# Queueing the casts of x and the first weight splits behind the PSUM copies of p's projections, in a hybrid decoder block on one Trainium2 core

## The chip, the core and the metric

The kernel runs on one core of one Trainium2 chip. The core has a matrix engine (TensorE, PE in the profile; PEld are its weight loads), VectorE (DVE), ScalarE (ACT), GpSimd (POOL) and SyncE (SP), which here only issues transfers. Matmul results land in PSUM, of which the kernel uses eight banks: four under the tag "g", four under "s". The metric is device time in microseconds, and lower is better.

## The reference

One layer of a decoder block on 256 tokens of width 2048, all in float32:

```
h = RMSNorm(x);  u = h @ W_in            # 12288 columns: c b xa za q f iv og ga gb
yA = (B * conv3(C * xa)) * silu(zA)      # short convolution
yB = HGRN2(silu(q), f, iv) normed * silu(og)
m  = sigmoid(ga) * (yA @ W_A) + sigmoid(gb) * (yB @ W_B);  x = x + m @ W_o
x  = x + sigmoid(RMSNorm(x) @ W_pg) * (p @ W_pp);  out = RMSNorm(x)
```

The last but one product, p @ W_pp (256 tokens, 256 deep, 2048 wide), depends on inputs alone, and this kernel computes it first.

## The kernel before

**Products.** A float32 matrix is used as two float32r parts, a rounded one (hi) and what is left (lo), and a product is three matmuls: hi by hi, hi by lo, lo by hi (`product`, lines 898 to 900). For weights, ScalarE makes the hi part (`whi`, line 123) and VectorE the lo part (`wlo`, line 124), in `split`. For x, `put` makes `xh` on ScalarE (line 215, which also applies the norm's gain) and `xl` on VectorE (line 216). In this text a cast is ScalarE's half of that, a split VectorE's.

**Positions and groups.** The weights are one stream of positions; a position is 256 rows by 512 columns of a weight matrix (512 KB) and takes 12 matmuls of 128x512: three for each of two row blocks and two token blocks. A group is 512 output columns, and uses two PSUM banks, one for each token block. Groups 0 to 3 are p's projections ("PP"), one position each (positions 0 to 3). Then come the input groups of eight positions each, the first at positions 4 to 11 (`FIRST = 4`), whose epilogue is `ep_f`. Projections 0 and 1 take all four "g" banks, projections 2 and 3 take "s" banks, and all input groups take "g" banks. So the first input group needs the banks of projection 0, the second those of projection 1.

**The copies.** The epilogue of a projection (`ep_pp`, lines 702 to 708) copies one bank out on ScalarE (line 704) and one on VectorE (line 705) to a tile, shown as `t`, and two steps later SP stores the tile to DRAM (`pw_d`, line 708). It is read back only with the last four groups (`load_pw`).

**The order.** Loop `for pos` first prepares weights until three positions ahead (`ahead`, LEAD = 3), then issues the position's matmuls, then lets each active epilogue go one step (`advance`). From position 4 on, preparing a position `done` also prepares two pieces of x (`put_x`, 128 features each, sixteen in all). The framework's scheduler then orders each engine's queue by its own estimates; an engine works through its queue strictly in that order. `tc.issue_after(i)` makes what is issued inside it stand behind instruction `i` on the engine that they share. `step` uses it so that an epilogue's instructions stand behind the last split. Before the change nothing tells the scheduler how the copies stand to the casts of x.

**Buffers and transfers.** `raw` holds two positions in each of three buffers, so positions 10 and 11 are loaded into the buffer of 4 and 5, and so on; `whi` and `wlo` have four buffers each, so position q's cast waits for the matmuls of position q - 4. SP issues all transfers in order: the first weights, x in eight pieces, weights of positions 6 to 9, then the stores to `pw_d`, further weights, four loads of x by tokens (`load_tokens`, line 802) and small masks (lines 943 and 944). The built program also lets a transfer wait for the landing of one eight before it.

**The norm of x.** ScalarE sums squares of the four token loads (`add_squares`, line 806), VectorE and GpSimd make rstd1 from it, and only then can `ep_f(0)` read the first group's banks (line 265), at position 18.

Of the kernel before, what the change touches and what calls it, by code (L numbers as in the profile page):

```python
# [11 lines left out]
AF = mybir.ActivationFunctionType  # L12
# [7 lines left out]
KT = D // P  # L20
# [3 lines left out]
CW = 512  # L24
# [21 lines left out]
def hybrid_kernel(ctx, tc, xT, x, pT, prm, gfin, masks, w_in, w_a, w_b, w_o, w_pg, w_pp, out):  # L46
    nc = tc.nc
# [11 lines left out]
    def open_pool(name, side):  # L59
        closers[name] = ExitStack()  # L60
        pools[name] = closers[name].enter_context(
            tc.tile_pool(name=name, bufs=1, side=side, reuse_waits="tile")
        )

    def close_pool(name):
        closers.pop(name).close()
        del pools[name]
# [3 lines left out]
    state = {"tmp": "tmp1"}  # L71
# [3 lines left out]
    def nm(s):  # L75
        uid[0] += 1
        return f"{s}_{uid[0]}"

    def t4(tag="t4", bufs=None):
        bufs = bufs or {"tmp1": 8, "tmp2": 5, "tmp3": 5}[state["tmp"]]  # L80
        return pools[state["tmp"]].tile([P, 1024], F32, tag=tag, bufs=bufs, name=nm(tag))
# [13 lines left out]
    def raw_of(pos):  # L95
        q = pos // 2
        if q not in loaded:
            loaded[q] = wp.tile([P, 2, 2 * CW], F32, tag="raw", bufs=3, name=nm("raw"))
        return loaded[q]

    def load(pos):
        q = pos // 2
        if q not in loaded:
            raw = raw_of(pos)
            w, g, c = stream[2 * q]
            if q < APART // 2:
                for i in range(2):
                    w, g, c = stream[2 * q + i]
                    nc.sync.dma_start(out=raw[:, i, :], in_=w[g, :, c, :])
            else:  # L110
                nc.sync.dma_start(out=raw, in_=w[g, :, c : c + 2, :])

    def split(pos, halves=(0, 1)):
        load(pos)
        src = raw_of(pos)[:, pos % 2, :]
        pool, n = (pools["late"], 6) if pos >= gate and (pos - gate) % 10 >= 4 else (wp, 4)
        if pos not in parts:
            parts[pos] = tuple(
                pool.tile([P, 2 * CW], F32R, tag=tag, bufs=n, name=nm(tag)) for tag in ("whi", "wlo")
            )  # L120
        hi, lo = parts[pos]
        s = slice(halves[0] * CW, (halves[-1] + 1) * CW)
        a = nc.scalar.activation(out=hi[:, s], in_=src[:, s], func=AF.Copy)  # L123
        v = nc.vector.tensor_tensor(  # L124
            out=lo[:, s], in0=src[:, s], in1=hi[:, s].bitcast(F32), op=ALU.subtract
        )
        state["splits"] = (a.ins, v.ins)
# [19 lines left out]
    FIRST = 4  # L147
# [11 lines left out]
    def load_x(k, n):  # L159
        nc.sync.dma_start(  # L160
            out=xraw[k // 4].rearrange("p (k t) -> p k t", k=4)[:, k % 4 : k % 4 + n, :], in_=xT[:, k : k + n, :]
        )
# [38 lines left out]
    def gain(base, k):  # L201
        return prm_t[:, base + k : base + k + 1]
# [5 lines left out]
    def put(op, k, src, scale=None):  # L208

        hi, lo = op[0][:, k, :], op[1][:, k, :]  # L210
        if scale is None:
            nc.scalar.activation(out=hi, in_=src, func=AF.Copy)
            nc.vector.tensor_tensor(out=lo, in0=src, in1=hi.bitcast(F32), op=ALU.subtract)
        else:
            nc.scalar.activation(out=hi, in_=src, func=AF.Identity, scale=scale)  # L215
            nc.vector.scalar_tensor_tensor(
                out=lo, in0=src, scalar=scale, in1=hi.bitcast(F32), op0=ALU.mult, op1=ALU.subtract
            )
# [482 lines left out]

    def ep_pp(j, psum):
        pw = t4()
        nc.scalar.activation(out=pw[:, :CW], in_=psum[0], func=AF.Copy)  # L704
        nc.vector.tensor_copy(out=pw[:, CW:], in_=psum[1])
        yield
        yield
        nc.sync.dma_start(out=pw_d[:, j, :], in_=pw)

    def load_pw(j):  # L710
        state["pw", j] = t4("pw", 2)
        nc.sync.dma_start(out=state["pw", j], in_=pw_d[:, j, :])
# [79 lines left out]
    def put_x(k):  # L792
        put(state["hT"], k, xraw[k // 4][:, (k % 4) * T : (k % 4 + 1) * T], gain(PRM_GMIX, k))
# [10 lines left out]
    def add_squares(q):  # L804

        tc.keep_in_program_order(nc.scalar.activation(
            out=xtok[q], in_=xtok[q], func=AF.Square, accum_out=state["ss1"][:, q : q + 1]
        ))

    def norm_of_x():  # L810
        tot = sc(NT, "tot1", 1)
        nc.vector.tensor_reduce(
            out=tot, in_=state["ss1"].rearrange("p (t h) -> p t h", t=NT),
            axis=mybir.AxisListType.X, op=ALU.add,
        )
        r = state["rstd1"] = rsqrt_of(tot, NT, D, "r1")
        state["rstd1_2"] = sc(NT, "r1s", 1)
        nc.vector.tensor_tensor(out=state["rstd1_2"], in0=r, in1=r, op=ALU.mult)
# [39 lines left out]
    def put_p(k):  # L858
        put(state["pT"], k, praw[:, k * T : (k + 1) * T])
# [14 lines left out]
    def step(e):  # L874

        a, v = state["splits"]
        with tc.issue_after(a), tc.issue_after(v):
            try:
                next(e)
            except StopIteration:  # L880
                active.remove(e)
# [9 lines left out]
    def ahead(pos):  # L891

        return LEAD + min(max(pos - gate, 0) // 4, 5)
# [9 lines left out]
    psum = None  # L903
    done = 0
    for pos, (gi, c) in enumerate(steps[:last_group]):
        kind, j, w, g, opname = groups[gi]
        nch = w.shape[2]
        if pos == gate:
            close_pool("m")
            open_pool("late", "left")  # L910
        while done < min(pos + 1 + ahead(pos), len(steps)):
            if done < 2:
                for i in range(2):
                    if done == 0:
                        put_p(i)
                    split(done, (i,))
            else:
                for k in range(2 * (done - FIRST), min(2 * (done - FIRST) + 2, KT)) if done >= FIRST else ():
                    put_x(k)
                split(done)  # L920
            done += 1
        if pos == 0:
            load(FIRST + 2)
            for k in (8, 10):
                load_x(k, 2)
            load(FIRST + 4)
            for k in (12, 14):
                load_x(k, 2)
        if pos >= gate and c == 0:
            load_pw(j)  # L930
        if pos == FIRST + 4:
            begin()
        if 0 <= pos - NORM < 4:
            add_squares(pos - NORM)
        if pos == NORM + 3:
            norm_of_x()
        if pos == NORM + 4:
            active.append(ep_f(0, waiting))
            step(active[-1])
            nc.gpsimd.memset(full_m, 0)  # L940
            for i in range(4):
                z = slice(i * Q, (i + 1) * Q)
                nc.sync.dma_start(out=near_m[z], in_=masks[z, :NARROW, z])
                nc.sync.dma_start(out=full_m[z, :, z], in_=masks[z, NARROW:, z])
        if c == 0:
            psum = [bank("s" if kind == "PP" and j >= 2 else "g") for _ in range(NT)]
        hi, lo = parts.pop(pos)
        for i in range(2):
            k = 2 * c + i
            s = slice(i * CW, (i + 1) * CW)  # L950
            for t in range(NT):
                product(psum[t], state[opname], k, t, hi[:, s], lo[:, s], k == 0, k == 2 * nch - 1)

        for q in range(done, min(done + AHEAD, len(steps)) if pos >= FIRST else 0):
            load(q)
        if 0 <= pos - TOKENS < 4:
            load_tokens(pos - TOKENS)
        advance()
        if kind == "O" and j == 0 and c == nch - 3:
            finish()  # L960
            third_part()
        if kind == "O" and j > 0 and c == 1:
            residual(j)
        if kind == "O" and j == 2 and c == 4:
            load_gfin()
        if c == nch - 1:
            if kind == "f" and j == 0:

                waiting = psum
                for n in ("yaT", "ybT"):  # L970
                    state[n] = operand(pools["branch"], n, DC // P)
            if kind == "ga" and j == 0:
                finish()
                second_part()
            if kind == "O" and j == 0:
                state["x1T"] = operand(big, "x", KT)
            if kind == "f" and j == 0:
                continue
            active.append(epilogues[kind](j, psum))
            step(active[-1])  # L980
# [5 lines left out]
    for t, halves in ((0, (0, 1)), (1, (0,)), (1, (1,))):  # L986
        bk, n = bank("g"), CW // 2
        for c in range(nlast):
# [4 lines left out]
            for i in range(2):  # L993
                k = 2 * c + i
# [84 lines left out]
```

## Time and profile before

| | |
|---|---|
| time, median of 3 runs | 831.6 us (831.57 to 832.35) |
| profiled execution, its own time | 832.67 us |
| span of that execution | 830.9 us |
| busy: PE, DVE, ACT | 816.6, 520.7, 438.0 us |
| mean granted clock of TensorE | 0.993 |
| moved by DMA | 186.72 MB, 225 GB/s |

The span is what the profiler recorded of one execution; the device time holds some 1.8 us around it. All rows come from that execution, and their times are from the span's start. A row of a timeline gives start and length in us, engine, line and operation, the output and input tiles (buffer numbers left out), and in brackets the idle time before it with what ended it; "xN" merges N in a row.

### The profile page before, as it was taken

The numbers are of one execution on the slowest core, as the hardware profiler recorded it, in microseconds if no ns is written. First come the engines' busy times: TensorE is split into PE (matmuls) and PEld (weight loads), VectorE is DVE, ScalarE is ACT, GpSimd is POOL, SyncE is SP. The second block draws the span as 40 slices with busy tenths as digits, with TensorE's granted clock in tenths as the row PEclk, the third lists the DMA queues.
The fourth block names the chain that finished last, engine by engine and source line by source line (L and its number), as shares of the span: only waits on it lengthen the run. The fifth ranks groups of instructions, "written<-read, shape, count | busy, mean of one in ns | idle before, by whom it ended". The sixth has DMA issues, their size and how long they took to land.

```text
span 830.9 us, 10483 instructions
## 1 busy us (share of the span) xinstructions
PE 816.6 (98%) x4104; PEld 676.3 (81%) x4104; DVE 520.7 (63%) x635; ACT 438.0 (53%) x578; POOL 35.6 (4%) x35
## 2 busy tenths in 40 slices
PE   7999999999999999999999999999999999999995
PEld 5788888888888888888888888888888888888885
DVE  6646678957776488767646545545644655676932
ACT  7456566466555476456543543444444445565623
POOL 1000000001000000000001000000100100000310
PEclk9899999999999999999999999999999999999998
DMA  9988565557877555648755755755756788778712
GB/s 336 326 283 294 198 203 201 152 207 227 276 235 234 197 197 183 223 153 263 238 192 172 254 198 203 254 184 185 244 198 202 241 278 291 261 269 330 252 54 102
DMA packets 42962, 186.72 MB, mean 225 GB/s; under 512 B 5920, under 2 KB 15392, under 8 KB 25120
## 3 DMA queue, kind: packets, MB, share of 16 engines
q1 hardware_dynamic: 42336, 185.00, 65.5%
q10 hardware_dynamic: 576, 1.05, 0.4%
q8 instruction: 32, 0.52, 0.3%
q14 instruction: 18, 0.15, 0.1%
HBM read 172.40 MB, written 13.63 MB: 224 GB/s over the span
## 4 chain that ended last, share of the span: by engine, by line
PE 95%; DMA 2%; issue 1%; ACT 1%; DVE 0%; SPq 0%; POOLq 0%; POOL 0%; ACTq 0%
PE g L898 31%; PE g L899 31%; PE g L900 31%; DMA raw<-in_w_in 1%; DMA raw<-in_w_pp 1%; PE s L425 1%; PE s L526 0%; PE s L544 0%; PE s L545 0%; PE s L543 0%; ACT xh L215 0%; ACT xs L761 0%; PE s L517 0%; ACT whi L123 0%; ACT t L744 0%
## 5 line engine op out<-in xcount | busy, mean ns | idle before, releaser
L124 DVE TENSOR_TENSOR wlo<-raw,whi 128x1024 fp32r<-128x1024 f32 (+1 forms) x294 | 360.9, 1234 | 267.9 <-ACT whi L123 265.8
L123 ACT ACTIVATE whi<-raw 128x1024 fp32r<-128x1024 f32 (+1 forms) x294 | 308.0, 1053 | 334.4 <-PE g L900 302.8
L898 PE MATMUL g<-whi,xh 128*128 128x512 f32 (+1 forms) x912 | 352.9, 387 | 4.4 <-ACT t L704 4.4
L899 PE MATMUL g<-wlo,xh 128*128 128x512 f32 (+1 forms) x912 | 352.6, 387 | 0.0
L900 PE MATMUL g<-whi,xl 128*128 128x512 f32 (+1 forms) x912 | 352.3, 386 | 0.0
L898 PEld LDWEIGHTS g<-whi,xh 128*128 128x128 f32 x912 | 172.1, 189 | 39.2 <-ACT t L704 4.8
L900 PEld LDWEIGHTS g<-whi,xl 128*128 128x128 f32 x912 | 172.1, 189 | 34.6
L899 PEld LDWEIGHTS g<-wlo,xh 128*128 128x128 f32 x912 | 172.1, 189 | 34.4
L899 PE MATMUL g<-wlo,mh 128*128 128x512 f32 x128 | 49.6, 389 | 0.0
L898 PE MATMUL g<-whi,mh 128*128 128x512 f32 x128 | 49.5, 389 | 0.0
L900 PE MATMUL g<-whi,ml 128*128 128x512 f32 x128 | 49.5, 389 | 0.0
L900 PEld LDWEIGHTS g<-whi,ml 128*128 128x128 f32 x128 | 24.0, 188 | 5.0
L899 PEld LDWEIGHTS g<-wlo,mh 128*128 128x128 f32 x128 | 24.0, 188 | 5.0
L898 PEld LDWEIGHTS g<-whi,mh 128*128 128x128 f32 x128 | 24.0, 188 | 4.9
L669 POOL TENSOR_TENSOR t<-ga,gb 128x512 f32<-128x512 f32 x8 | 14.1, 1792 | 262.2 <-DVE gb L665 262.2
L900 PE MATMUL g<-whi,yaTl 128*128 128x512 f32 x64 | 24.9, 389 | 0.0
L898 PE MATMUL g<-whi,yaTh 128*128 128x512 f32 x64 | 24.9, 389 | 0.0
L899 PE MATMUL g<-wlo,yaTh 128*128 128x512 f32 x64 | 24.9, 389 | 0.0
L898 PE MATMUL g<-whi,ybTh 128*128 128x512 f32 x64 | 24.9, 389 | 0.0
L899 PE MATMUL g<-wlo,ybTh 128*128 128x512 f32 x64 | 24.9, 389 | 0.0
L900 PE MATMUL g<-whi,ybTl 128*128 128x512 f32 x64 | 24.9, 389 | 0.0
L257 DVE STREAM_TRANSPOSE t<-t 128x1024 f32<-128x1024 f32 x16 | 19.8, 1239 | 0.3 <-DMA t<-turn 0.2
(161 smaller groups left out, 468.5 us busy)
## 6 DMA issues: line engine op xcount, KB each, us to landing
raw<-in_w_in SPq DMA_DIRECT2D x90, 1024.0 KB, 5.0
raw<-in_w_o SPq DMA_DIRECT2D x16, 1024.0 KB, 6.6
raw<-in_w_pg SPq DMA_DIRECT2D x16, 1024.0 KB, 6.3
turn<-t SPq DMA_DIRECT2D x72, 128.0 KB, 2.6
t<-turn SPq DMA_DIRECT2D x18, 512.0 KB, 5.1
raw<-in_w_a SPq DMA_DIRECT2D x8, 1024.0 KB, 5.1
raw<-in_w_b SPq DMA_DIRECT2D x8, 1024.0 KB, 5.1
raw<-in_w_in SPq DMA_DIRECT2D x10, 512.0 KB, 7.4
```

The costliest lines, as they stand in the source:

```text
L123: a = nc.scalar.activation(out=hi[:, s], in_=src[:, s], func=AF.Copy)
L124: v = nc.vector.tensor_tensor(out=lo[:, s], in0=src[:, s], in1=hi[:, s].bitcast(F32), op=ALU.subtract)
L257: nc.vector.transpose(out=dst.rearrange("p (k a e) -> p a k e", a=4, e=32), in_=src.rearrange("p (a k e) -> p a k e", a=4, e=32))
L425: nc.tensor.matmul(out, X[:, 0, h, s], X[:, 1, h, t], start=True, stop=True, tile_position=(0, i * n))
L669: nc.gpsimd.tensor_tensor(out=spread(m, t), in0=blocks(ga[:, s]), in1=blocks(gb[:, s]), op=ALU.add)
L898: nc.tensor.matmul(psum, oh, hi, start=first, stop=False)
L899: nc.tensor.matmul(psum, oh, lo, start=False, stop=False)
L900: nc.tensor.matmul(psum, ol, hi, start=False, stop=last)
```

## The change

```diff
@@ ep_pp
     def ep_pp(j, psum):
         pw = t4()
-        nc.scalar.activation(out=pw[:, :CW], in_=psum[0], func=AF.Copy)
-        nc.vector.tensor_copy(out=pw[:, CW:], in_=psum[1])
+        a = nc.scalar.activation(out=pw[:, :CW], in_=psum[0], func=AF.Copy)
+        v = nc.vector.tensor_copy(out=pw[:, CW:], in_=psum[1])
+        state["copied"] = (a.ins, v.ins)
         yield
         yield
         nc.sync.dma_start(out=pw_d[:, j, :], in_=pw)
@@ for pos, ...: while done < min(pos + 1 + ahead(pos), len(steps))
             else:
-                for k in range(2 * (done - FIRST), min(2 * (done - FIRST) + 2, KT)) if done >= FIRST else ():
-                    put_x(k)
-                split(done)
+                with ExitStack() as behind:
+                    for i in state["copied"] if done >= FIRST else ():
+                        behind.enter_context(tc.issue_after(i))
+                    for k in range(2 * (done - FIRST), min(2 * (done - FIRST) + 2, KT)) if done >= FIRST else ():
+                        put_x(k)
+                    split(done)
             done += 1
```

`ep_pp` now keeps its two copies. When position `done` (4 or later) is prepared, its pieces of x and its cast and split are issued behind the copies kept last: position 4 behind those of projection 0, position 5 behind projection 1's, position 6 behind 2's, position 7 and all later ones behind 3's. Instructions, tiles and transfers are the same ones as before.

In the queues as built this gives, on ScalarE and on VectorE, four rounds of copy, two pieces of x and one position's cast or split, then four positions with two pieces of x each. On SP the order after the last piece of x becomes: first store, two loads of `near_m` with one of `full_m` between them, second store, weights of positions 10 and 11, third and fourth store, weights of positions 12 and 13, then 14 and 15. Before, it was two stores, weights of 10 and 11, third store, weights of 12 and 13, fourth store, weights of 14 and 15, and all mask loads later.

## The prediction

> **What bounds the kernel now.** I read the page's shares first, then who made TensorE wait, then the first 36 us engine by engine. The page:
>
> ```profile
> span 830.9 us, 10483 instructions
> PE 816.6 (98%) x4104; PEld 676.3 (81%) x4104; DVE 520.7 (63%) x635; ACT 438.0 (53%) x578; POOL 35.6 (4%) x35
> ```
>
> TensorE (PE) is busy for 816.6 of 830.9 us, so only two things can shorten the span: fewer idle stretches of PE, or matmuls that are paced faster. The view of waits, for PE alone (total us, times, longest):
>
> ```profile
> PE g L898 <- ACT t L704: 4.4, 1, 4.4
> ```
>
> Besides the start this is PE's only listed wait: one matmul waits 4.4 us for line 704, ScalarE's copy of p's projection out of PSUM. PE's timeline shows where (start us, us, engine, line, operation, [idle before]):
>
> ```profile
> 16.74 0.39 PE L900 MATMUL s<-whi,pop 128*128 128x512 f32 x1
> 21.49 0.80 PE L898 MATMUL g<-whi,xh 128*128 128x512 f32 x1 [4.37 <-ACT t L704]
> 27.89 0.40 PE L898 MATMUL g<-whi,xh 128*128 128x512 f32 x1
> 30.19 0.39 PE L899 MATMUL g<-wlo,xh 128*128 128x512 f32 x1
> 35.86 0.39 PE L900 MATMUL g<-whi,xl 128*128 128x512 f32 x1
> ```
>
> The last matmul of the projections starts at 16.74, the first input group's first at 21.49. From 30.19 to 35.86 are 25 matmuls, so the pitch is 0.227 us and a position of 12 matmuls takes 2.72. The stretches of the clock (length; PE, weight loads, DVE, ACT, POOL busy with counts; granted clock; DMA share; GB/s):
>
> ```profile
> 7.20:14.03 6.83, 6.83 (x32) 5.65 (x31) 5.06 (x6) 4.94 (x8) 0.00 (x0) 1.00 1.03 380
> 14.03:20.85 6.82, 3.10 (x14) 2.24 (x12) 6.82 (x12) 6.63 (x13) 0.00 (x0) 1.00 1.04 406
> 20.85:27.68 6.83, 6.19 (x15) 4.84 (x16) 5.38 (x12) 4.33 (x10) 0.00 (x0) 0.50 0.90 298
> 27.68:34.50 6.82, 6.82 (x32) 5.61 (x30) 2.97 (x3) 2.52 (x3) 0.00 (x0) 1.00 0.99 346
> ```
>
> After the gap the granted clock is 0.50 for 6.83 us, and the 15 matmuls in it, from 21.49 to 27.89, take 6.40 us. So the gap costs twice. Why the copies are late, on ScalarE's and VectorE's timelines:
>
> ```profile
> 10.34 1.06 ACT L123 ACTIVATE whi<-raw 128x1024 fp32r<-128x1024 f32 x1 [0.41 <-DMA raw<-in_w_pp]
> 11.70 1.06 ACT L123 ACTIVATE whi<-raw 128x1024 fp32r<-128x1024 f32 x1 [0.30 <-PE g L900]
> 12.67 0.89 ACT L215 ACTIVATE xh<-t,prm_t 128x256 fp32r<-128x256 f32 x2
> 14.68 2.49 ACT L215 ACTIVATE xh<-t,prm_t 128x256 fp32r<-128x256 f32 x6
> 17.08 1.04 ACT L123 ACTIVATE whi<-raw 128x1024 fp32r<-128x1024 f32 x1
> 18.31 1.06 ACT L123 ACTIVATE whi<-raw 128x1024 fp32r<-128x1024 f32 x1 [0.19 <-DMA raw<-in_w_in]
> 20.87 1.05 ACT L704 ACTIVATE t<-g 128x512 f32<-128x512 f32 x2
> 21.82 1.07 ACT L704 ACTIVATE t<-s 128x512 f32<-128x512 f32 x2
> 11.43 2.58 DVE L124 TENSOR_TENSOR wlo<-raw,whi 128x1024 fp32r<-128x1024 f32 x2 [0.25 <-ACT whi L123]
> 13.94 0.88 DVE L216 SCALAR_TENSOR_TENSOR xl<-t,prm_t,xh 128x256 fp32r<-128x256 f32 x2
> 14.81 1.22 DVE L124 TENSOR_TENSOR wlo<-raw,whi 128x1024 fp32r<-128x1024 f32 x1
> 15.95 2.46 DVE L216 SCALAR_TENSOR_TENSOR xl<-t,prm_t,xh 128x256 fp32r<-128x256 f32 x6
> 18.33 2.35 DVE L124 TENSOR_TENSOR wlo<-raw,whi 128x1024 fp32r<-128x1024 f32 x2
> 21.79 1.28 DVE L705 COPY t<-g 128x512 f32<-128x512 f32 x2
> 22.98 1.27 DVE L705 COPY t<-s 128x512 f32<-128x512 f32 x2
> ```
>
> The four copies stand behind twelve casts of x and four casts of weights that TensorE doesn't need yet. Projections 0 and 1 hold all four "g" banks, so the first input group cannot start.
>
> **The change part by part.** Nothing is added or removed in arithmetic; it is an order. In the changed kernel as built each copy stands first in a round, on ScalarE and on VectorE alike: copy of projection j, two pieces of x (2j and 2j+1), cast and split of position 4+j. From position 8 on there are no copies, and x is spread two pieces to a position. TensorE's order stays, but for a swap inside the first position.
>
> Costs, as start-to-start in the rows above. ScalarE: weight cast 0.97 (11.70 to 12.67), piece of x 0.40 (six from 14.68 to 17.08), copy 0.475 (two from 20.87 to 21.82): a round is 0.475 + 0.80 + 0.97 = 2.25 us. VectorE: split 1.14 (14.81 to 15.95), piece 0.40 (six from 15.95 to 18.33), copy 0.60 (two from 21.79 to 22.98): 0.60 + 0.80 + 1.14 = 2.54 us. Both are under PE's 2.72 us, so a round keeps up once it has a lead.
>
> The lead, walked through. I take a piece of x as there when ScalarE cast it before (12.67, 14.68), which is late if anything. Projection 0's last matmul is 36 before that of 16.74, so at 8.6; ScalarE's first copy follows the cast of 10.34 at 11.31. x 12.67, position 4's cast 13.47, done 14.53. VectorE: copy 12.57 (its second split of the row of 11.43 is 1.14 long), x 13.17, split 14.55, done 15.77. PE wants it at 16.74 + 0.23 = 16.97: 1.2 us spare. Then by rounds:
>
> ```
> position  ScalarE copy, x, cast   VectorE split done   PE wants it   spare
> 4         11.31, 12.67, 13.47     15.77                16.97         1.2
> 5         14.44, 14.92, 15.72     18.3                 19.69         1.4
> 6         16.69, 17.17, 17.97     20.85                22.41         1.6
> 7         18.94, 19.42, 20.22     23.4                 25.13         1.7
> ```
>
> The copies of projections 1 to 3 find their matmuls done (11.7, 14.4 and 17.1 at 12 x 0.227 each, back from 16.74 + 0.39), so no queue stands still for PE. With the whole durations instead of the pitches a VectorE round is at most 0.68 + 0.95 + 1.22 = 2.85 us, and the last spare is still about 0.8. What the move adds, the later first split (15.8 instead of about 14), is covered by projections 2 and 3, which keep PE busy till 17. Bounds of this part: 0 with the cover, 1.8 us lost if that cover were gone.
>
> The gain then has two terms. The gap: 21.49 - 16.97 = 4.52 us. The clock: 15 matmuls at the full pitch are 15 x 0.227 = 3.40 us instead of 6.40, so 3.00 us. Sum 7.52. Bounds: 4.5 (the clock falls anyway, or does not fall in the timed runs of before) and 7.6. I take 7.5: with no gap there is nothing for the low stretch to stand behind, since of the stretches shown only the one after the gap has 0.50, and the two before it 1.00.
>
> [...]
>
> **The transfers that move.** The copies being early, SP issues the four stores to pw_d earlier and ahead of input weights; three small mask loads move between them too. Rows on SP and landings (KB, us from issue to landing; each landing row is of the issue above it):
>
> ```profile
> 15.66 0.33 SPq L160 DMA_DIRECT2D t<-in_xT  x1
> t<-in_xT SPq DMA_DIRECT2D x1, 256.0 KB, 7.8
> 22.53 0.33 SPq L708 DMA_DIRECT2D pw_d<-t  x1
> pw_d<-t SPq DMA_DIRECT2D x1, 512.0 KB, 2.7
> 32.89 1.06 SPq L109 DMA_DIRECT2D raw<-in_w_in  x1
> raw<-in_w_in SPq DMA_DIRECT2D x1, 512.0 KB, 7.6
> near_m<-in_masks SPq DMA_DIRECT2D x1, 16.0 KB, 4.7
> 26.00:30.00 4.00, 4.00 (x16) 3.18 (x15) 1.46 (x2) 1.06 (x1) 0.00 (x0) 0.79 0.98 248
> ```
>
> Everything issued before the stores lands by 15.66 + 7.8 = 23.5, as now, for the stores stand behind it. Between the first store's landing (25.2) and position 15's weights (40.5) nine pieces of 512 KB landed: 1.70 us each. In the changed order position 12's first weights are the seventh piece: 23.5 + 7 x 1.70 = 35.4, plus 48 KB of masks, about 0.2. Position 12 starts on PE at 16.97 + 8 x 2.72 = 38.7, and cast and split need 2.3 us: they must land by 36.4. Spare 0.8, the narrowest of the run-in. If the masks cost three SP issues instead (0.4 each), the spare is gone but nothing is lost yet.
>
> **The rivals.**
> 1. *The gap goes, the clock term doesn't* (the timed runs never had the low stretch, or it moves elsewhere). For: one profiled run only, and 832.67 against a median of 831.6. Against: the three runs lie within 0.8 us, less than the 3.0 the term would scatter. 4.5 us gained: 827.1. [...]
> 2. *Casts late.* If PSUM reads slow down next to a PE at full clock, say the copies on VectorE take double, four rounds add 4 x 0.6 = 2.4 against 1.7 spare: 0.7 lost, 824.8; with 1.8 lost, 825.9. Against: those copies ran from 21.79 on beside a running PE.
> 3. *Loads late a little* at position 12 or 13: 1 us lost, 825.1.
> 4. *Slower: transfers become the bound.* The stores ahead of the weights push the whole queue. From the first store to the fourth token load of x are 20 pieces of 512 KB. That load feeds the squares, rstd1 and the read of group f(0)'s banks, which the third input group needs at position 20 (16.97 + 16 x 2.72 = 60.5 in the changed kernel):
>
> ```profile
> 61.05 1.04 ACT L806 ACTIVATE t<-t 128x1024 f32<-128x1024 f32 x1
> 63.77 1.25 ACT L265 ACTIVATE t<-g,r1r 128x512 f32<-128x512 f32 x2
> ```
>
> From square to banks free are 63.77 + 1.25 - 61.05 = 4.0 us, so it must land by 56.5: (56.5 - 23.5)/20 = 1.65 us a piece. At the 248 GB/s of the slowest stretch throughout, a piece takes 2.11 and it lands at 65.7, 9.2 late: 1.7 us slower than before, 833.3. It decides from 2.03 us a piece (258 GB/s). Against: the row of 27.68 moved 346 GB/s, and 248 lasted 4 us.
> 5. *Nothing happens*: the first input group waits for something else until 21.5. Against: its weights and x are split by 15 (second split of the row of 11.43, and the row of 13.94), and it starts 0.05 us after the first copy's end (20.87 + 0.57). 831.6.
>
> **How the numbers follow.** Profiled execution 832.67 (span 830.9): I expect 825.2 and 823.4. The median of the runs shown, 831.6, is 1.1 below the profiled one; less 7.5 it gives 824.1. Chances: this forecast 0.74, rival 1 0.09, rival 2 0.06, rival 3 0.06, rival 4 0.03, rival 5 0.02. The likeliest one's own range is 823.4 to 825.0; to take in rivals 1 to 3 the range is 823.3 to 827.2. A measurement of this kernel can tell about 0.2% (1.7 us) from no change. Faster by more than that: 0.74 + 0.09 + 0.06 + 0.06 = 0.95; slower 0.03; same 0.02.
>
> **What would show it.** Right: PE's wait for line 704 gone; the first "g<-whi,xh" matmul at about 17.0; clock 1.00 from 7.2 us to the end of the matmuls; PE's starts 7.5 us earlier from 30 us to the end, and no new PE wait over 0.5 us. The VectorE split of position 4 done at 15.4 to 15.8; the first store issued near 17 instead of 22.5. Wrong: a PE wait for "wlo" between 17 and 28 (rival 2), for "whi" with a DMA behind it near 38 to 42 (rival 3), for ScalarE's line 265 near 60 (rival 4), or a stretch of clock 0.50 after 17 us (rival 1).

## The result and the profile after

| | before | changed |
|---|---|---|
| time, median of 4 runs each | 831.59 us (831.05 to 832.35) | 825.17 us (824.62 to 825.37) |
| span of the profiled execution | 830.9 us | 823.3 us |
| mean granted clock in it | 0.993 | 0.998 |

The ratio is 0.9921, 95% interval 0.9904 to 0.9938: 6.4 us faster. In a second comparison, with 4 runs of the changed kernel and 27 of the one before on the same chip, it was 824.88 against 832.04 us, 0.9915 (0.9901 to 0.9929): 7.2 us. The forecast was 824.1, and 823.4 to 825.0 for the likeliest course: the first median lies 0.2 us outside, the second inside. By the time alone rivals 2 and 3 (824.8 and 825.1) would fit as well; the rows have to decide.

The head of the changed kernel's page, and all that the view of waits lists for TensorE:

```profile
span 823.3 us, 10487 instructions
PE 813.3 (99%) x4104; PEld 674.1 (82%) x4104; DVE 520.2 (63%) x635; ACT 437.4 (53%) x578; POOL 35.6 (4%) x35
```

```profile
PE s L791 <- DVE warm L787: 1.5, 1, 1.5
```

The wait for line 704 is gone and no other has come; what is left is the start. TensorE's timeline (start us, us), where the last projection meets the first input group, and 50 matmuls on:

```profile
16.69 0.39 PE L901 MATMUL s<-whi,pop 128*128 128x512 f32 x1
16.92 0.62 PE L899 MATMUL g<-whi,xh 128*128 128x512 f32 x2
...
28.25 0.39 PE L901 MATMUL g<-whi,xl 128*128 128x512 f32 x1
```

The same 50th matmul started at 35.86 before: 7.6 us, and the two spans differ by 7.6 too, so nothing was given back later. The stretches of the clock (length; busy times with counts; granted clock; DMA share; GB/s) that read 3.10 busy and 0.50 before:

```profile
14.03:20.85 6.82, 6.82 (x32) 5.65 (x31) 6.71 (x10) 6.82 (x14) 0.00 (x0) 1.00 1.04 407
20.85:27.68 6.83, 6.83 (x32) 5.66 (x31) 6.74 (x12) 4.23 (x8) 0.00 (x0) 1.00 1.04 393
```

And the four rounds on VectorE (splits of positions 4 to 7), ScalarE's first copy, the first store, and ScalarE's casts of positions 10 and 12:

```profile
11.26 0.58 ACT L704 ACTIVATE t<-g 128x512 f32<-128x512 f32 x1
28.64 1.06 ACT L123 ACTIVATE whi<-raw 128x1024 fp32r<-128x1024 f32 x1 [3.56 <-DMA raw<-in_w_in]
33.64 1.06 ACT L123 ACTIVATE whi<-raw 128x1024 fp32r<-128x1024 f32 x1 [2.19 <-DMA raw<-in_w_in]
14.14 1.23 DVE L124 TENSOR_TENSOR wlo<-raw,whi 128x1024 fp32r<-128x1024 f32 x1
16.68 1.22 DVE L124 TENSOR_TENSOR wlo<-raw,whi 128x1024 fp32r<-128x1024 f32 x1
19.20 1.21 DVE L124 TENSOR_TENSOR wlo<-raw,whi 128x1024 fp32r<-128x1024 f32 x1
21.73 1.22 DVE L124 TENSOR_TENSOR wlo<-raw,whi 128x1024 fp32r<-128x1024 f32 x1
16.95 0.33 SPq L709 DMA_DIRECT2D pw_d<-t  x1
```

The splits end at 15.4, 17.9, 20.4 and 22.95, where 15.8, 18.3, 20.85 and 23.4 were forecast. Position 12's weights were there at 33.6; 35.4 was forecast and 36.4 needed.

### The profile page after: what moved, and what is told of

It reads as the page before. It is cut to its first block, busy times and chain, and to the rows that moved or that the text cites. A ratio compares the mean times of both kernels' runs of the same rounds, so it can differ in the third digit from the quotient of the medians.

```text
span 823.3 us, 10487 instructions
## 1 busy us (share of the span) xinstructions
PE 813.3 (99%) x4104; PEld 674.1 (82%) x4104; DVE 520.2 (63%) x635; ACT 437.4 (53%) x578; POOL 35.6 (4%) x35
## 4 chain that ended last, share of the span: by engine, by line
PE 97%; issue 1%; ACT 0%; DVE 0%; POOLq 0%; POOL 0%
PE g L899 32%; PE g L900 32%; PE g L901 32%; PE s L425 1%; PE s L791 0%; PE s L526 0%; PE s L901 0%; PE s L900 0%; PE s L899 0%; PE s L545 0%; PE s L544 0%; PE s L543 0%; ACT xs L762 0%; PE s L517 0%; ACT t L745 0%
```

## The experiments

**Both kernels again, run by run.** No edit.

> The kernel before, unchanged, to see its spans and granted clocks run by run. Theory P (the place of the half-clock stretch moves from run to run, and this is why the profiled gain of 7.6 us was above the 6.4 us of the medians): the runs' mean clocks differ (0.993 where all 6.8 us of the stretch lie behind the gap; up to 0.998 where a part lies in the gap), and the time falls by about 0.4 us for each 0.0005 of clock; spread about 831.0 to 832.7 us. Rival (something fixed outside the span): all clocks 0.993, spans equal within 0.2 us, and device time minus span differs from the changed kernel's 2.0 us.

> The changed kernel, unchanged, beside the one above. Theory P: no half-clock stretch before the tail in any run, clocks 0.997 to 0.998, times 824.5 to 825.4, a spread of half of that of the kernel before; median gain 6.0 to 7.6 us. Rival: the gain is 6.4 with both spreads under 0.3 us.

Before: 831.45 us (830.91 to 832.75) in 11 runs, and 27 more runs of the same program in the same comparison. Changed: 824.88 (824.56 to 825.21). The runs' spans, by their mean clock:

```
before, 38 runs  clock 0.992 and 0.993: 28 runs, mean span 830.4   clock 0.994: 10 runs, 829.4
changed, 4 runs  clock 0.998: 2 runs, 823.1                        clock 0.997: 2 runs, 822.55
```

Theory P holds in kind: the unchanged kernel's spans reach from 829.0 to 831.7 us, and 1.0 us of that lies between the two groups of clock; the changed one's reach from 822.5 to 823.2. The clocks differ by less than Theory P expected (0.992 to 0.994), and within a group of one clock the spans still differ by up to 2 us, which stays unexplained. The stretches of this second execution of the kernel before, cut every 3.41 us from the steps of its clock (21.16 and 24.57):

```profile
14.33:17.75 3.42, 2.27 (x11) 1.53 (x9) 3.05 (x7) 3.42 (x8) 0.00 (x0) 1.00 1.03 410
17.75:21.16 3.41, 0.00 (x0) 0.00 (x0) 3.41 (x7) 3.24 (x7) 0.00 (x0) 1.00 1.04 404
21.16:24.57 3.41, 2.95 (x7) 2.40 (x8) 3.41 (x8) 3.41 (x8) 0.00 (x0) 0.50 0.69 266
```

Here the clock is 0.50 for 3.41 us, in the first execution it was for 6.83. The first input group started at 21.62 and 21.49, so the start hardly moves, but the cost of the clock does: from the first matmul to the 50th behind it are 14.37 us in the first execution and 12.85 in the second (21.62 to 34.47), against 11.33 in the changed kernel, so 3.04 and 1.52 us. In the changed kernel the difference of 0.6 us lies ahead of the input groups: in the execution of span 823.3 they start at 16.92, in that of 822.6 at 16.27.

The rival has a grain of truth. Device time less span is 1.78 us (mean of the 38 runs) before and 2.05 for the changed kernel: 0.27 us of the gain is lost outside the span, where no trace shows anything.

**The gap filled, the copies left late.** Zeros are added to the sums, so the result is the same, and only TensorE's idle time goes.

```diff
-                product(psum[t], state[opname], k, t, hi[:, s], lo[:, s], k == 0, k == 2 * nch - 1)
+                if pos == FIRST - 1 and (i, t) == (1, NT - 1):
+                    for _ in range(18):
+                        nc.tensor.matmul(psum[t], warm[:, :P], warm, start=False, stop=False)
+                product(psum[t], state[opname], k, t, hi[:, s], lo[:, s], k == 0, k == 2 * nch - 1)
```

> The kernel before with 18 matmuls of zeros added in front of the last product of projection 3 (they add nothing to its sums), so that the gap is filled and the copies stay late. Theory (the gap costs twice, by itself and by the clock): the first input group still starts at about 21.5 us, the clock is 1.00 from 7 us on, and only the clock term goes: 3.0 us faster in the profile, about 828.6 us (828.0 to 829.6). Rival (the low stretch is no answer to the idle gap, or zeros do not count): the clock still falls to 0.50 and the time stays at 831.6.

830.28 us, ratio 0.9979 (0.9970 to 0.9987): 1.8 us, not 3.0, though no run's clock was under 0.996. The experiment had a fault. ScalarE's timeline, a cast and then the first copies:

```profile
20.85 1.06 ACT L124 ACTIVATE whi<-raw 128x1024 fp32r<-128x1024 f32 x1 [0.45 <-PE s L901]
...
22.21 1.06 ACT L705 ACTIVATE t<-g 128x512 f32<-128x512 f32 x2
```

Position 7's cast takes position 3's buffer, which the held-back products kept until 20.8; the copies behind it came at 22.21 instead of 20.87. So the zeros were put behind the last product instead, 20 of them, and in a second kernel 10:

```diff
-                product(psum[t], state[opname], k, t, hi[:, s], lo[:, s], k == 0, k == 2 * nch - 1)
+                fill = pos == FIRST - 1 and (i, t) == (1, NT - 1)
+                product(psum[t], state[opname], k, t, hi[:, s], lo[:, s], k == 0, k == 2 * nch - 1 and not fill)
+                if fill:
+                    for n in range(FILL):  # FILL = 20, 10
+                        nc.tensor.matmul(psum[t], warm[:, :P], warm, start=False, stop=n == FILL - 1)
```

> The kernel before with 20 matmuls of zeros behind the last product of projection 3, in its last bank (they add nothing to the sums). Unlike the first filler they don't hold back the products, so position 7's cast and ScalarE's copies keep their places. Theory (the clock term is the low stretch behind the gap, 1.5 to 3.0 us by where the gap lies in the clock's windows): the first input group starts at 21.4 to 21.5, the clock is 1.00 from 7 us to the tail, the 50th matmul behind the first starts at about 32.9 where before it was 34.5 to 35.9; 2.2 us faster, 829.2 to 830.2 us. Rival (the term is always 3.0): 828.9. Rival (no clock term): 831.9.

829.48 us, ratio 0.9973 (0.9964 to 0.9983), against 831.87 as the mean of the 17 runs beside it: 2.35 us from the mean of 829.52. The zeros (19 of the 20 are in the trace), the first input group and the 50th matmul behind it on TensorE's timeline:

```profile
17.13 4.26 PE L957 MATMUL s<-warm 128*128 128x512 bf16 x19
...
21.38 0.50 PE L899 MATMUL g<-whi,xh 128*128 128x512 f32 x1
...
32.86 0.39 PE L901 MATMUL g<-whi,xl 128*128 128x512 f32 x1
```

The copies are as late as before (ScalarE's first at 20.76), the clock stays at 1.00, and the 50th matmul is at 32.9, as was worked out, instead of 34.5 to 35.9. This is the clock term by itself, 2.35 us in the mean. The rest of the way to the changed kernel is the gap: mean span 827.72 against 822.83 (from another comparison), 4.9 us, or 5.1 when each is taken against the mean of the kernel before in its own comparison (830.07 and 830.30).

> The same with 10 matmuls of zeros, so that TensorE idles for about 2.3 us instead of 4.5 before the first input group. Theory (the clock falls behind a window of 3.41 us of which TensorE was busy for less than about 2 us): in some four of five runs most of the gap lies in one window, the clock falls, and only a part of the term is saved: 830.3 to 831.7 us, with runs of different clocks. Rival (only a window that is idle throughout lowers the clock): no low stretch in any run, 2.2 us faster like the full filler.

Two groups: five runs of 829.3 to 829.5 us at clock 0.996 to 0.997, three of 831.0 to 831.9 at 0.995. In the second group the clock was lower, in three of eight runs where four of five were expected. Of these a trace was kept of one; there the wait for the copies was 2.5 us, and from 23.52 on the clock was 0.50 for 3.41 us, so it fell here behind an idle stretch well under 3.41 us:

```profile
16.69:20.11 3.42, 2.79 (x13) 1.12 (x12) 3.42 (x8) 3.25 (x6) 0.00 (x0) 1.00 1.04 405
20.11:23.52 3.41, 1.47 (x6) 1.23 (x7) 3.41 (x7) 3.41 (x9) 0.00 (x0) 1.00 0.74 284
23.52:26.93 3.41, 3.41 (x9) 2.65 (x8) 3.29 (x8) 2.11 (x5) 0.00 (x0) 0.50 0.78 302
```

**One half of the constraint.** The first kernel keeps only VectorE's copy in what is waited for:

```diff
-        state["copied"] = (a.ins, v.ins)
+        state["copied"] = (v.ins,)
```

> The change with the casts and splits behind the VectorE copies alone: as built VectorE's queue is that of the changed kernel and ScalarE's that of the kernel before. Theory (the gap is set by ScalarE's copy of projection 0): the first input group starts at 21.4 to 21.5 us and the time is that of before, 831.6 within 0.5. Rival (half of the gain comes from VectorE): 828.

832.23 us, ratio 1.0005 (0.9996 to 1.0015): no gain. VectorE's first copy ran at 12.29, ScalarE's at 20.62 behind the casts; TensorE's wait:

```profile
PE g L899 <- ACT t L704: 4.8, 1, 4.8
```

With the constraint on ScalarE alone, or on projection 0's copies alone, the built program has the same queues on every engine as the changed kernel, so these were not run. To get VectorE's copies late they were issued three steps on:

```diff
-        v = nc.vector.tensor_copy(out=pw[:, CW:], in_=psum[1])
-        state["copied"] = (a.ins, v.ins)
+        state["copied"] = (a.ins,)
         yield
+        yield
+        yield
+        nc.vector.tensor_copy(out=pw[:, CW:], in_=psum[1])
+        yield
         yield
```

> The change with ScalarE's copies early and VectorE's copies issued three positions later, behind the splits of positions 4 to 6. Theory (both halves of projection 0 have to be out, so the later copy sets the start): by the changed kernel's rows VectorE's first copy ends at about 20.4 us, the first input group makes one matmul at 16.9 and goes on at 20.4 to 20.6; the gap of about 3.2 us costs 3.3, and where the clock falls behind it, up to 3.0 more: 828.3 without, 831.0 with the fall. Rival (ScalarE's copy alone matters): 825.2.

824.84 us, ratio 0.9910 (0.9894 to 0.9927): the theory fell, the rival's number came. Rows of VectorE and of TensorE:

```profile
19.52 0.68 DVE L709 COPY t<-g 128x512 f32<-128x512 f32 x1
```

```profile
16.51 0.62 PE L902 MATMUL g<-whi,xh 128*128 128x512 f32 x2
```

TensorE starts both token blocks at 16.51, three microseconds ahead of VectorE's first copy. So neither bank of the first input group can be one that VectorE empties. In the built programs the framework gave this group the two banks that ScalarE empties, of projections 0 and 1, here and in the kernel before the change; in the changed kernel, and in the one with VectorE's copies alone early, it gave it both banks of projection 0, one emptied by ScalarE and one by VectorE. The text above, that the first input group needs the two banks of projection 0, holds for these last two alone. So the run doesn't test the theory's condition: with VectorE late the framework chose banks that don't need it.

**The stores doubled and more.** Two more stores per projection, into a buffer that nothing reads:

```diff
         nc.sync.dma_start(out=pw_d[:, j, :], in_=pw)
+        for n in range(2):
+            nc.sync.dma_start(out=pw_e[:, n, j, :], in_=pw)
```

> The changed kernel with each of the four stores of p's projections issued three times (the two more into a buffer that nothing reads): eight pieces of 512 KB more ahead of the weights of positions 14 and 15, six more ahead of those of position 12. Theory (the transfers behind 23.5 us are one queue at 1.44 us a piece, as position 12's weights landing at 33.6 as the seventh piece show, with a spare of 2.8 us there): position 14's weights are the 17th piece and land at 48.0 where 41.9 is wanted, so TensorE loses about 6 us, in waits before positions 10, 12 and 14: 831. At the 1.70 us a piece of the forecast it is 52.4, 10.5 us lost: 835.7. Rival (stores run beside the loads and cost the weights nothing): 825.2.

829.11 us, ratio to the kernel before 0.9965 (0.9952 to 0.9978): 4.2 us slower than the changed kernel (824.88, from another comparison), where about 6 were expected. ScalarE's casts of positions 10, 12 and 14, and the stretches around TensorE's waits:

```profile
33.25 1.06 ACT L123 ACTIVATE whi<-raw 128x1024 fp32r<-128x1024 f32 x1 [7.25 <-DMA raw<-in_w_in]
39.54 1.06 ACT L123 ACTIVATE whi<-raw 128x1024 fp32r<-128x1024 f32 x1 [1.73 <-DMA raw<-in_w_in]
45.85 1.06 ACT L123 ACTIVATE whi<-raw 128x1024 fp32r<-128x1024 f32 x1 [3.97 <-DMA raw<-in_w_in]
```

```profile
31.69:35.10 3.41, 1.69 (x7) 0.83 (x5) 0.76 (x1) 1.61 (x2) 0.00 (x0) 1.00 1.02 418
35.10:38.52 3.42, 2.90 (x7) 2.32 (x8) 3.04 (x9) 0.71 (x2) 0.00 (x0) 0.50 1.03 420
```

In this program the fourth store and its copies stand behind the weights of 12 and 13, so these casts wait for the 7th, 12th and 17th piece behind 23.5 us. They start at 33.25, 39.5 and 45.9; at 1.44 us a piece it would be 33.6, 40.8 and 48.0. So the queue of transfers is the mechanism, at 1.3 to 1.4 us a piece, and the stores did stand in the way of the loads (position 10's cast at 33.25 instead of 28.64). TensorE waited twice, 1.48 us for the cast and 0.76 us for the split of position 10, and 0.50 of the clock for 3.42 us came on top; before positions 12 and 14, where waits were expected too, it had none.

**VectorE's copies made three times.**

```diff
-        v = nc.vector.tensor_copy(out=pw[:, CW:], in_=psum[1])
+        for _ in range(3):
+            v = nc.vector.tensor_copy(out=pw[:, CW:], in_=psum[1])
```

> The changed kernel with each VectorE copy made three times over, 1.2 us more in each of four rounds, so that VectorE's round is 3.7 us against TensorE's 2.72. Theory (the changed kernel has 1.6 to 2.2 us of spare in the rounds, by its rows): position 4 still starts at 16.9, position 7's split is done at about 27.6 where 25.6 is wanted, 1.5 to 2.2 us lost: 827.0, with TensorE waiting for wlo before positions 6 and 7. Rival (later rounds take it back, or PSUM reads overlap more than the pitch says): 825.2.

828.19 us, ratio to the kernel before 0.9951 (0.9936 to 0.9966): 3.3 us more than the changed kernel (824.88, from another comparison), where 1.5 to 2.2 were expected. TensorE's wait (us in total, times, longest), and VectorE's first two sets of copies:

```profile
PE g L901 <- DVE wlo L124: 2.6, 3, 0.9
```

```profile
12.18 2.13 DVE L706 COPY t<-g 128x512 f32<-128x512 f32 x3
...
16.16 2.13 DVE L706 COPY t<-g 128x512 f32<-128x512 f32 x3
```

The round is 3.98 us, not 3.7, for copies of one tile follow each other at about 0.7 us (2.13 us for the three). TensorE then loses 3.98 - 2.72 = 1.26 us a round once the lead is used up: its waits end at 20.27, 24.24 and 28.21, 3.97 us apart. The direction and the cause, waits for "wlo", are the theory's; there were three of them where two were expected.

## Why the prediction held, and where its terms were off

- *The wait.* TensorE sat idle for ScalarE's copies behind casts that were not yet needed: shown by the wait that went, and by the kernel with VectorE's copies alone early, which kept it (4.8 us) and gained nothing.
- *The gap term*, forecast at 4.52 us: 4.57 in the profiled pair (21.49 to 16.92), 5.35 in the second (21.62 to 16.27), 4.9 to 5.1 between the filled and the changed kernel's mean spans. Right, if a little low.
- *The clock term*, forecast at 3.00: 3.04 in the first profile and 1.52 in the second, 2.35 in the mean of the filled kernel's runs, since the low stretch was 6.83 us long in the one traced execution and 3.41 in the other. This term was mis-sized: it was read from one execution. Rival 1 doubted that the timed runs had the term, but put it at all or nothing; it is a matter of size.
- *The sum*, forecast at 7.52: the span changed by 7.6 in the first profiled pair, by 6.9 in the second (829.5 to 822.6; 5.35 and 1.52 make 6.87) and by 7.5 in the mean of the second comparison (830.30 to 822.83). That the mean is met so closely is in part luck: its gap term is larger than forecast by about as much as its clock term is smaller.
- *Outside the span*, forecast at nothing: 0.27 us lost, so that 7.5 of the mean span is 7.2 in the times. The 6.4 us of the first comparison rests on four runs each of kernels of which the one before scatters over 2.7 us; its interval, 5.2 to 8.0 us, takes in both.
- *The rounds* kept up with 0.4 us more to spare than worked out, as x landed earlier than its casts before had shown (12.25 against 12.67). Rival 2 did not happen: a round on VectorE took the 2.5 us of the forecast (16.68 to 19.20 to 21.73), and TensorE waited for no "wlo". It needs more than the 0.6 us a round that it was given: 1.4 us more cost 3.3 us.
- *The transfers.* Position 12 had 2.8 us to spare, not 0.8: a piece took 1.44 us (33.6 less 23.5, over seven), for 1.70 had been measured over a stretch (25.2 to 40.5) in which the DMA moved 321 GB/s; in the changed kernel it moved 404 from 16.9 to 33.6. Why the first was slower is not shown. Rival 3 did not happen, and neither did rival 4: line 265 read the first group's banks at 56.17, 7.6 us earlier than before. That stores hold up the weights behind them is real, as the extra stores show, but eight more pieces cost 4.2 us and did not undo the gain.
- *Which copies matter.* The prediction made all four copies and both engines part of the cause. With ScalarE's copies early and VectorE's late the gain was the same, since the framework then picked banks that ScalarE empties; VectorE's half of the constraint changes nothing in the built queues.

## What to carry to other kernels

Look at what stands in an engine's queue ahead of the instruction that frees a buffer: here 0.5 us of copying, of a bank whose last matmul ended by 8.97, stood until 20.87 behind work that could wait, and held the busiest engine for 4.6 to 5.4 us. The idle gap of TensorE cost its length here and then 1.5 to 3 us more at half clock, differing from execution to execution, so size such a term from several profiles. And before arguing over which of several constraints works, compare the built queues: VectorE's half of this one, or the parts for projections 1 to 3, could each be left out.

## What the hardware showed that was not expected

In these traces the low stretch was 3.41 or 3.42 us long (the second execution before, the kernel with 10 matmuls of zeros, the one with more stores) or 6.83, twice that (the first execution before, from which the prediction had its length, and the kernel with VectorE's copies alone early). Cut into windows of 3.41 us from the steps of the clock, they also show it falling behind windows that were not idle throughout. Rows from the kernel with VectorE's copies alone early:

```profile
15.70:19.11 3.41, 0.70 (x4) 0.24 (x2) 3.41 (x7) 3.22 (x7) 0.00 (x0) 1.00 1.03 400
19.11:22.52 3.41, 1.27 (x3) 1.08 (x4) 3.41 (x6) 3.41 (x9) 0.00 (x0) 0.50 1.03 398
22.52:25.94 3.42, 3.42 (x9) 2.65 (x9) 0.80 (x3) 1.75 (x5) 0.00 (x0) 0.50 1.03 316
25.94:29.30 3.36, 3.36 (x16) 2.75 (x16) 1.70 (x3) 1.11 (x2) 0.00 (x0) 1.00 0.87 250
```

Read with the rows above: the clock fell behind windows with TensorE busy for 0.00, 0.70, 1.47 and 1.69 us, and stayed behind 2.27 and 2.79. From 0.50 it was back at 1.00 behind windows with 2.90 and 2.95 us of work, and still 0.50 behind one with 1.27. In the first execution before, it was still 0.50 behind the window from 20.85 too:

```profile
20.85:24.27 3.42, 2.78 (x7) 2.20 (x8) 3.42 (x8) 3.42 (x9) 0.00 (x0) 0.50 0.77 294
24.27:27.68 3.41, 3.41 (x10) 2.64 (x9) 1.97 (x5) 0.91 (x2) 0.00 (x0) 0.50 1.04 302
```

So in the windows shown the clock fell behind at most 1.69 us of work in 3.41 and stayed behind 2.27 and more; it came back behind 2.90 and more, and not behind 2.78. The busy times are modelled ends, so all four are rough. This fits the two lengths of the low stretch: the first input group started 0.64 us into its window in the one execution (21.49 after 20.85), which left 2.78 us of work in it, and 0.46 in the other (21.62 after 21.16), which left 2.95. In these two executions of one kernel the clock fell at 20.85 and 21.16, 3.72 and 4.56 us after the projections' last matmul ended (17.13 and 16.60).
